# Row sums on one core: the early results leave by fifteen stores of 9, 15, 14, ... 2 partitions instead of one store of 128

## The chip, the core and the metric

The kernel runs on one core of a Trainium2 chip. Its time is the device time of one execution in microseconds (us). The kernel before takes 160.73 us, the median of three runs that lie between 160.67 and 160.77. Four engines appear below: VectorE (DVE), ScalarE (ACT), GpSimd (POOL, which does nothing here but set constants) and SyncE (SP), which issues every transfer of this kernel. The transfers themselves are carried by the core's 16 DMA engines.

## The reference

The input is 32 x 512 rows of 1024 float32 numbers, 67.1 MB. Each row is summed and the sum multiplied by 0.5, so the output has 16,384 numbers, 65.5 KB.

```python
def reference(x, multiplier):            # x: (32, 512, 1024) float32, multiplier 0.5
    return (np.sum(x, axis=-1) * multiplier).astype(np.float32)
```

## The kernel before, in words

The 16,384 rows are cut into eight blocks of 16 rows for each of the 128 partitions. In the first seven blocks a partition owns 112 rows that follow one another in memory (`own = rows - B`, lines 42 to 45), so in the output a partition's 112 results are 448 contiguous bytes. The eighth block is another part of the input, 16 rows for each partition, and its results are 64 contiguous bytes for each partition. The results of both parts lie in one tile, `res`, columns 0 to 111 and 112 to 127.

Three buffers `xb` of 8.4 MB each take the blocks in turn. SP issues the load of a block as one transfer of 128 x 64 KB (line 75, helper `load`); from the fourth block on the load waits until VectorE is done with the buffer's previous block (the semaphore `dve_done`). The first three loads are moved to the program's entry, ahead of the barrier there, by the function at the end (`start_loads_at_entry`).

VectorE sums blocks 0 to 5 with one reduction over 16 rows each (line 117) and scales the sums into `res` (line 123). Of block 6 it sums 8 rows, and ScalarE the other 8, one row at a time (`act_row`, line 82), straight into `res`. With that the 112 early columns are complete.

The last block is loaded in five pieces, all issued by SP as soon as the buffer is free (lines 139 to 148): rows 0 to 7, 8 to 12, 13 to 14, and row 15 in two parts of 608 and 416 numbers in a tile of its own, `end`. VectorE (`dve_sum`, line 92) and ScalarE share the rows. The two parts of row 15 are VectorE's: `first` (line 167) sums the first part when it has landed, `final` (line 170) adds the second part and writes the last column of `res`. `final` waits for the second part's landing and for `first` on one semaphore.

After the five loads SP waits for the early columns (lines 149 and 151: VectorE's through `dve_done`, ScalarE's through `act_done`) and issues the early store, `out_rows <- res[:, 0:own]`, 128 x 448 bytes, as one transfer (line 150). It then waits for ScalarE's last row (line 174) and for `final`, and issues the last store, `out_last <- res[:, own:]`, 128 x 64 bytes (line 175). At the end it waits for both stores (lines 179 and 180, one instruction in the trace, under line 180). The order on SP is the order in the source; no scheduler changes it. All loads and stores are issued on SP's one queue, and each has a semaphore of its own that counts to 16 when the transfer has landed.

Of the kernel before, what the change touches and what calls it, by code (L numbers as in the profile page):

```python
# [9 lines left out]
def kernel(  # L10
# [13 lines left out]
    nc = tc.nc  # L24
# [4 lines left out]
    P = nc.NUM_PARTITIONS  # L29
# [12 lines left out]
    own = rows - B  # L42
    x_rows = x_flat[0 : P * own, :].rearrange("(p c) d -> p c d", p=P)
    x_last = x_flat[P * own : N, :].rearrange("(p c) d -> p c d", p=P)
    out_rows = out_flat[0 : P * own].rearrange("(p c) -> p c", p=P)
    out_last = out_flat[P * own : N].rearrange("(p c) -> p c", p=P)

    def sbuf(name, *shape):
        return ctx.enter_context(nc.sbuf_tensor(name, list(shape), fp32)).ap()
# [4 lines left out]
    res = sbuf("res", P, rows)  # L54
# [4 lines left out]
    def sem(name):  # L59
        return nc.alloc_semaphore(name=name)  # L60

    dve_done = sem("dve_done")
    act_done = sem("act_done")
    counts = {"dve": 0, "act": 0}

    def marks(i, engine):

        s = dve_done if engine == "dve" else act_done
        i.then_inc(s, 1)
        counts[engine] += 1  # L70
        return counts[engine]
# [33 lines left out]
    for b in range(n_blocks - 1):  # L105
# [12 lines left out]
                out=sums[:, c0 : c0 + h], in_=t[:, 0:h, :], axis=mybir.AxisListType.X  # L118
# [5 lines left out]
            out=res[:, c0 : c0 + h],  # L124
            in_=sums[:, c0 : c0 + h],
# [5 lines left out]
        if h < B:  # L131
# [3 lines left out]
            early_act = marks(i, "act")  # L135
# [11 lines left out]
        for k, (to, lo, hi) in enumerate(((0, 0, cut), (at, cut, D)))  # L147
    ]
    nc.sync.wait_ge(dve_done, early_dve)
    early = nc.sync.dma_start(out=out_rows, in_=res[:, 0:own])  # L150
    early.wait_op(act_done, early_act, "sem-ge")
    early_stored = sem("early_stored")
    early.then_inc(early_stored, 16)

    on_act = {4, 5, 6, 7, 11, 12, 14}
    for k, (lo, hi) in enumerate(pieces):
# [19 lines left out]
    store.wait_op(dve_done, done, "sem-ge")  # L176
    stored = sem("stored")
    store.then_inc(stored, 16)
    nc.sync.wait_ge(early_stored, 16)
    nc.sync.wait_ge(stored, 16)  # L180

    def start_loads_at_entry(nc_):
# [61 lines left out]
```

## Time and profile before

| What | Value |
|---|---|
| Time, median of three runs | 160.73 us (160.67 to 160.77) |
| Span of the profiled execution | 159.4 us; the profile gives it no other time of its own, so what lies around the span is read as the difference to the median, 1.3 us |
| DVE busy | 119.3 us, 75% of the span |
| ACT busy | 17.3 us, 11% |
| DMA packets | 2016, 67.18 MB, mean 421 GB/s; 98.0% of 16 engines' span |
| of these under 512 B | 480 |
| Early store, SP's issue | starts at 146.96 us, 0.35 us long, landed 10.8 us after its start |
| Last store, SP's issue | starts at 157.97 us, 0.34 us long, landed 1.4 us after its start |

The span runs from the first to the last instruction that the profile shows. A transfer has two entries: the instruction on SP's queue (SPq) that issues it, some 0.35 us, and the time from there to its landing, when its semaphore is full. A transfer is carried as packets: here one packet for each partition's contiguous run and one 4-byte packet for each increment of the semaphore. Fourteen transfers of 128 packets and 16 increments make the 2016.

### The profile page before, as it was taken

To read this page: it belongs to the slowest core of one execution; us is meant where nothing else is said; L and a number is where in the kernel's file an instruction comes from. 1 tells how busy PE (TensorE), PEld (TensorE's weight loads), DVE (VectorE), ACT (ScalarE), POOL (GpSimd) and SP (SyncE) were. 2 spreads that over 40 slices of the span, in tenths; PEclk is the share of its full clock that TensorE was granted. 3 is DMA by queue.
4 is the path that set the end of the run, shared out by engine and by line. 5 is a ranking of instruction groups with operands and counts; after the bars stand their busy time and mean duration, and the time that the engine had idled before them with its cause. 6 is when DMAs were issued, how large, how long until landed. Compare 5 with 4: busy or idle time off the path is not lost.

```text
span 159.4 us, 122 instructions
## 1 busy us (share of the span) xinstructions
DVE 119.3 (75%) x35; ACT 17.3 (11%) x31; POOL 0.2 (0%) x4
## 2 busy tenths in 40 slices
DVE  0000059998699978999599995999959999598644
ACT  3000000000000000000000000000000000397954
POOL 0000000000000000000000000000000000000000
DMA  7996996996999979969969969969979799698994
GB/s 263 526 526 263 526 510 280 526 510 280 526 395 395 526 312 477 526 296 493 526 263 526 526 263 526 510 280 526 477 312 526 345 444 526 280 501 364 421 410 145
DMA packets 2016, 67.18 MB, mean 421 GB/s; under 512 B 480, under 2 KB 608, under 8 KB 736
## 3 DMA queue, kind: packets, MB, share of 16 engines
q1 hardware_dynamic: 2016, 67.18, 98.0%
HBM read 67.11 MB, written 0.07 MB: 421 GB/s over the span
## 4 chain that ended last, share of the span: by engine, by line
DMA 76%; DVE 22%; SPq 1%; issue 0%
DMA xb<-in_x_dram 51%; DMA end<-in_x_dram 25%; DVE sums L117 22%; SPq L75 1%; DVE end L92 1%; DVE res L123 0%; DVE res L92 0%
## 5 line engine op out<-in xcount | busy, mean ns | idle before, releaser
L117 DVE TENSOR_REDUCE sums<-xb 128x16 f32<-128x16384 f32 (+1 forms) x7 | 112.0, 16001 | 30.9 <-DMA xb<-in_x_dram 30.9
L82 ACT ACTIVATE xb<-xb 128x1024 f32<-128x1024 f32 x15 | 15.7, 1044 | 137.7 <-DMA xb<-in_x_dram 137.7
L92 DVE CUSTOM_DVE_ANT_0 xb<-xb 128x512 f32<-128x512 f32 x8 | 5.1, 688 | 4.9 <-DMA xb<-in_x_dram 4.9
L82 ACT ACTIVATION_READ_ACCUMULATOR xb<-xb 128x1 f32 x15 | 2.8, 186 | 0.0
L103 DVE MEMSET end<- 128x2 f32 x1 | 0.1, 60 | 2.5 <-PEq L26 2.5
L82 ACT ACT_TABLE_LOAD x1 | 1.3, 1283 | 2.4 <-PEq L26 2.4
L123 DVE TENSOR_SCALAR res<-sums 128x16 f32<-128x16 f32 (+1 forms) x7 | 1.2, 174 | 0.2
L92 DVE CUSTOM_DVE_ANT_0 end<-end 128x304 f32<-128x304 f32 (+1 forms) x2 | 0.9, 426 | 0.1
L92 DVE DVE_READ_ACCUMULATOR2_ANT res<- 128x1 f32 x9 | 0.7, 82 | 0.0
L225 POOL MEMSET const-bfloat16-1.0<- 128x1 bf16 x1 | 0.1, 102 | 0.0
L225 POOL MEMSET const-uint8-127<- 128x1 uint8 x1 | 0.1, 102 | 0.0
L225 POOL MEMSET const-float32-1.0<- 128x1 f32 x1 | 0.1, 99 | 0.0
L225 POOL MEMSET const-float32-0.0<- 128x1 f32 x1 | 0.1, 98 | 0.2 <-issue 0.2
L92 DVE DVE_READ_ACCUMULATOR2_ANT end<- 128x1 f32 x1 | 0.1, 81 | 0.0
## 6 DMA issues: line engine op xcount, KB each, us to landing
xb<-in_x_dram SPq DMA_DIRECT2D x1, 4096.0 KB, 31.2
xb<-in_x_dram SPq DMA_DIRECT2D x1, 2560.0 KB, 36.9
xb<-in_x_dram SPq DMA_DIRECT2D x1, 1024.0 KB, 38.9
end<-in_x_dram SPq DMA_DIRECT2D x1, 304.0 KB, 39.1
end<-in_x_dram SPq DMA_DIRECT2D x1, 208.0 KB, 39.2
xb<-in_x_dram SPq DMA_DIRECT2D x7, 40.8
out_dram<-res SPq DMA_DIRECT2D x1, 56.0 KB, 10.8
out_dram<-res SPq DMA_DIRECT2D x1, 8.0 KB, 1.4
```

The source lines that it names most:

```text
L75: i = nc.sync.dma_start(out=dst, in_=src)
L82: return nc.scalar.activation(out=t[:, r, :], in_=t[:, r, :], func=mybir.ActivationFunctionType.Copy, scale=mul, accum_out=res[:, col : co ...
L92: return nc.vector.tensor_tensor_reduce(out=row[:, 0:mid], in0=row[:, 0:mid], in1=row[:, mid:], scale=scale, scalar=0.0, op0=ADD, op1=ADD, ...
L103: marks(nc.vector.memset(end[:, at - 2 : at], 0.0), "dve")
L117: nc.vector.reduce_sum(out=sums[:, c0 : c0 + h], in_=t[:, 0:h, :], axis=mybir.AxisListType.X),
L123: scaled = nc.vector.tensor_single_scalar(out=res[:, c0 : c0 + h], in_=sums[:, c0 : c0 + h], scalar=mul, op=mybir.AluOpType.mult,)
L225: nc = _bacc.Bacc("TRN2", target_bir_lowering=False, num_devices=1)
```

## The change

The one early store becomes a loop of fifteen stores. Each takes the next n partitions of the same columns, with n = 9, 15, 14, 13, ... 3, 2, which adds up to 128. The first keeps the wait for ScalarE; the wait for VectorE stands ahead of the loop as before. All count up the same semaphore, and the wait at the end asks for 16 x 15 = 240. The bytes written and their addresses are the same, and nothing else in the kernel changes; VectorE, ScalarE and GpSimd have the same instructions in the same order, and SP has fourteen transfers more between the last load and the last store.

```diff
     nc.sync.wait_ge(dve_done, early_dve)
-    early = nc.sync.dma_start(out=out_rows, in_=res[:, 0:own])
-    early.wait_op(act_done, early_act, "sem-ge")
     early_stored = sem("early_stored")
-    early.then_inc(early_stored, 16)
+    early_parts = [9] + list(range(15, 1, -1))
+    assert sum(early_parts) == P
+    p0 = 0
+    for n in early_parts:
+        early = nc.sync.dma_start(
+            out=out_rows[p0 : p0 + n, :], in_=res[p0 : p0 + n, 0:own]
+        )
+        if p0 == 0:
+            early.wait_op(act_done, early_act, "sem-ge")
+        early.then_inc(early_stored, 16)
+        p0 += n
...
-    nc.sync.wait_ge(early_stored, 16)
+    nc.sync.wait_ge(early_stored, 16 * len(early_parts))
     nc.sync.wait_ge(stored, 16)
```

## The prediction

> **What bounds the kernel now.** I read the page's head and its DMA queue first, then the chain of work that ended last, in order of time, for the end of the kernel.
>
> ```profile
> span 159.4 us, 122 instructions
> ...
> q1 hardware_dynamic: 2016, 67.18, 98.0%
> ```
>
> The queue is full for 98% of the span, so the input's 67.1 MB set the time, and only what happens after the last load can be added or taken away by a store.
>
> ```profile
> 117.88 39.13 DMA end<-in_x_dram
> 157.01 0.02 issue
> 157.03 0.50 DVE end L92 x2
> 157.54 0.02 issue
> 157.56 0.38 DVE end L92
> 157.94 0.01 DVE res L92
> ```
>
> The first part of row 15 lands at 157.01 and releases `first`. `final` starts at 157.56, 0.04 us after `first` is done (157.03 + 0.50 = 157.53) and as close behind the landing of the second part (issued 0.48 us after the first part, 39.2 us to landing, so 157.5 to 157.6): the two are a tie. The last store is issued at 157.97 and lands 1.4 us later, at 159.4. The early store isn't on this chain. The next two views, the queue of SP and the issues with their landings, say how far off it is.
>
> ```profile
> SPq L149 <- DVE res L123: 28.1, 1, 28.1
> ...
> SPq L174 <- ACT xb L82: 10.1, 1, 10.1
> SPq L180 <- DMA out_dram<-res: 1.1, 1, 1.1
> SPq L175 <- DVE res L92: 0.5, 1, 0.5
> ```
>
> ```profile
> end<-in_x_dram SPq DMA_DIRECT2D x1, 304.0 KB, 39.1
> end<-in_x_dram SPq DMA_DIRECT2D x1, 208.0 KB, 39.2
> ...
> out_dram<-res SPq DMA_DIRECT2D x1, 56.0 KB, 10.8
> out_dram<-res SPq DMA_DIRECT2D x1, 8.0 KB, 1.4
> ```
>
> After issuing the early store SP is idle for 10.1 us and then 0.5 us. The store, issued at 146.96, lands 10.8 us later, at about 157.8, though the last store needs 1.4: its packets stand behind the loads on every DMA engine. Stretches of the end show the room behind them (columns: stretch and length, busy time of DVE, ACT and POOL, clock, DMA share of 16 engines, GB/s).
>
> ```profile
> 154.00:157.00 3.00, 2.40 (x8) 2.70 (x5) 0.00 (x0) 1.00 0.96 379
> 157.00:157.30 0.30, 0.27 (x1) 0.30 (x2) 0.00 (x0) 1.00 0.15 39
> 157.30:158.80 1.50, 0.60 (x4) 0.12 (x2) 0.00 (x0) 1.00 0.00 0
> 158.80:159.10 0.30, 0.00 (x0) 0.00 (x0) 0.00 (x0) 1.00 0.31 28
> ```
>
> The queue is empty from 157.3, when the early store's packets end, to 158.8, when those of the last store begin: 1.5 us in which all 16 engines do nothing.
>
> **The change, part by part.** Issuing. SP gets fourteen transfers more. The timeline has the prices:
>
> ```profile
> 116.51 1.32 SPq L75 DMA_DIRECT2D xb<-in_x_dram  x3
> 117.88 0.94 SPq L75 DMA_DIRECT2D end<-in_x_dram  x2
> 146.96 0.35 SPq L150 DMA_DIRECT2D out_dram<-res  x1
> 157.97 0.34 SPq L175 DMA_DIRECT2D out_dram<-res  x1
> ```
>
> An issue that stands alone takes 0.35 us, one in a row 0.44 to 0.47 (0.94 / 2). Fifteen take between 15 x 0.35 = 5.3 and 15 x 0.47 = 7.1 us; I take the latter, since they stand in a row, and SP is through at 146.96 + 7.1 = 154.0. Queued behind them on SP is only the wait of line 174, which ends with ScalarE's last row at 157.4, and the last store, due at 157.97. The cover is 3.4 us to the first; it would be gone at (157.97 - 146.96) / 15 = 0.73 us for one issue. Cost 0.
>
> Room for what is issued. By the trace's packets, when the fifth piece had been issued at 118.82, 848 packets were queued and not started, 53 on each engine, in six transfers. With the change the load of rows 13 and 14 and the two parts of row 15 are still queued at 154.0, at most 27 packets on each engine, and on top come 128 stores' packets and at most 240 increments, 23 for each engine if evenly spread: 50. So the packets fit in what was held before; the number of transfers, 18 against six or seven, was never tried here. Cost 0, and a rival.
>
> Packets. On the engine that ends last, the trace has the early store's packets of 448 bytes 21 ns apart and an increment 6 ns ahead of what follows. Eight and one increment took 8 x 21 + 6 = 174 ns. How a store of 9 or 15 partitions is laid on the engines no row shows. Evenly, nothing but the increments grows. If every store takes one packet on each engine from the same first one, the fullest engine has fifteen of each: 15 x 27 = 405 ns, 0.23 more. If all went to one engine, 128 x 21 + 15 x 6 = 2.8 us, from 157.1 to 159.9, 1.1 us past the start of the last store's packets. I take 0.23, because all fourteen transfers of the trace are spread over the engines (224 increments, 16 for each); it lies in the 1.5 us of empty queue. Less than before isn't to be had, since those packets aren't on the chain. Cost 0, at worst 1.1.
>
> The Trainium skill, DMA: Bandwidth & Descriptors, section "Why a DMA increments its semaphore by 16 and not by 1", says that a transfer uses the largest number of engines up to 16 that divides its outer dimension, the lowest-numbered ones. By that rule the fullest engine has fifteen stores' packets and engines post 128 increments; the sum is the same. No run here shows it yet.
>
> Landing of the loads. The last increments of row 15's second part hold up `final`, and the fifteen stores put up to 128 increments, if one per packet, beside them instead of 16. The landings in the trace bound the price. The last store's sixteen increments land exactly 10 ns apart, though several were issued within 3 ns; around the early store no two, of store or load, land less than 11 ns apart; but those of earlier loads come as little as 3 ns apart. If all pass through one line at 12 ns in the order of issue, replaying the packets with fifteen to none on the engines puts the last load's increment 0.1 to 0.53 us later, by which engine ends last. If the engines take turns, 15 x 12 = 0.18 us is the most. If the counter takes one in 3 ns, nothing. The straggler's load increment landed 0.43 us after its packet in the midst of store increments that took 0.52, so it did not stand behind them all: I take 0.05 us, near the lower end, and keep 0 and 0.53.
>
> The end. The last wait now asks for 240. Issued packets end by about 157.5 and increments land by 158.8 even at 12 ns each, before the last store's at 159.4. Cost 0; the 1.3 us around the span are unchanged.
>
> Sum, against the profiled execution's 159.43 us of span and 1.30 us to the median of the runs: 159.43 + 1.30 + 0 + 0 + 0 + 0.05 + 0 = 160.78 us. No difference under 0.2%, 0.32 us, can be told from no change here.
>
> **The rivals.** (1) The crowd of increments, the other side: with one line at 10 to 12 ns in order of issue, `final` and the last store start 0.32 to 0.53 us late, 161.05 to 161.26. It decides from about 27 increments (0.32 / 0.012) ahead of the straggler's. For it: the spacing above; against it: the straggler's 0.43 us. (2) Stores that go one at a time on an engine, each waiting for its increment to land. The trace has 0.50 us from the straggler's increment packet of the early store to its landing. Fifteen take 7.5 us from 157.0, so the last store's packets start at 164.5 instead of 158.8: 166.4. It decides from (158.8 - 157.0) / 15 = 0.12 us for one. Against it: after a load's increment the next packet starts 6 ns later, and an early store's increment was issued 175 ns after a load's on the same engine while that was in flight. The Trainium skill, Perfetto Trace Analysis, section "DMA Instruction — HWDGE (DVE, Sync)", says that the increment waits for the write and that this can be surprisingly long towards HBM; the trace agrees only in part, 0.50 for the store against 0.43 for the load. (3) A limit on transfers in flight. With four loads still out at 147.7 and each landing setting one free, a limit of 15 or more costs nothing; at eight, seven stores are issued only after 157.9, 7 x 0.35 to 0.44, so 2.5 to 3.1 us: 163.2 to 163.8. (4) A short store's issue costs more than 0.73 us; at 1.0 SP is through at 162.0, 4 us late: 164.8. (5) Faster: the straggler carries less behind its loads. But its loads stand ahead of the stores, and if its two last landings came with the other engines', about 0.15 us sooner, `first` would still wait for VectorE's row before, which ends at 156.97, and gain 0.06, `final` 0.04 more: 160.63, within the 0.2%. More than that needs a shorter landing of the last store, which no row suggests.
>
> **How the numbers follow.** The forecast and the small gain of (5) together 0.63, own range 160.6 to 161.0; (1) 0.17; (2) 0.05; (3) 0.07; (4) 0.02; a gain over 0.32 us by something unseen 0.06. Same 0.63, slower 0.31, faster 0.06. The range 160.5 to 161.4 holds the forecast's cases and (1) with its upper bound, 0.80.
>
> **What the profile after would show.** Fifteen issues on SP from 146.96, 0.35 to 0.47 each, through by 154; SP's wait for ScalarE's last row still there, some 3 us; the last store's issue within 0.1 us of 157.97 and 1.4 us to landing; more packets under 512 B. Against me: an issue of the last store after 158.3 with `final` late (1) or SP busy until then (3, 4), or a landing of the last store over 1.7 us after its issue (2).

## The result, and the profile after

The kernel with fifteen stores takes 161.75 us, the median of four runs (161.63 to 162.0), against 160.74 us for the kernel before: a ratio of 1.0065, 95% interval 1.005 to 1.0079. It is 1.0 us slower. The profiled execution took 161.79 us; its span is 160.5 us, 1.05 longer than before.

The page of the changed kernel: the queue carries 112 packets more, which are increments (128 for the fifteen stores, where the one had 16).

```profile
span 160.5 us, 136 instructions
...
DMA packets 2128, 67.18 MB, mean 419 GB/s; under 512 B 592, under 2 KB 720, under 8 KB 848
...
q1 hardware_dynamic: 2128, 67.18, 97.4%
```

The end of its chain of work, in order of time (start, length, what):

```profile
117.80 39.10 DMA end<-in_x_dram
156.89 0.02 issue
156.91 0.51 DVE end L92 x2
157.42 0.02 issue
157.45 0.38 DVE end L92
157.82 0.01 DVE res L92
```

Nothing is late up to here. The two parts of row 15 land as before, and `final` is done 0.12 us earlier than before, which is the spread of two executions. Its timeline and the issues with their landings (last column) show SP's side:

```profile
146.84 5.43 SPq L155 DMA_DIRECT2D out_dram<-res  x15
...
157.86 0.36 SPq L183 DMA_DIRECT2D out_dram<-res  x1
```

```profile
out_dram<-res SPq DMA_DIRECT2D x1, 8.0 KB, 2.6
```

SP is through with the fifteen stores at 152.3 and issues the last store at 157.86. But this store, with the same 8 KB, lands 2.6 us after its issue instead of 1.4. That is the whole loss: -0.11 for the earlier issue, +1.16 for the later landing, 1.05 together. The queue of SP says the same as a wait:

```profile
SPq L182 <- ACT xb L82: 5.1, 1, 5.1
SPq L188 <- DMA out_dram<-res: 2.2, 1, 2.2
SPq L183 <- DVE res L92: 0.5, 1, 0.5
```

The wait at the end was 1.1 us and is 2.2. The last view is the one that decides. In stretches of the end (DVE, ACT, POOL busy, clock, DMA share, GB/s) the DMA engines are hardly busier than before (a share of 0.23 against 0.15 in the first stretch, then none as before):

```profile
157.00:157.30 0.30, 0.30 (x1) 0.30 (x2) 0.00 (x0) 1.00 0.23 48
157.30:158.70 1.40, 0.48 (x4) 0.01 (x1) 0.00 (x0) 1.00 0.00 0
158.70:159.00 0.30, 0.00 (x0) 0.00 (x0) 0.00 (x0) 1.00 0.31 28
159.00:160.50 1.50, 0.00 (x0) 0.00 (x0) 0.00 (x0) 1.00 0.00 0
```

The packets of the early stores end at 157.30, and those of the last store start at 158.71 and end at 158.92. Then no packet moves for 1.5 us, and the kernel waits. What is late isn't data but the increments of the semaphores. The trace records when each one lands. The last packet of an early store's increment started at 157.30, but the last of these increments landed at 160.25; the last increment of the last store landed at 160.43. From 159.3 on the landings come in groups of six, six, five, three, one and one, 0.18 to 0.21 us from the start of one group to the next. That fits engines that each land one increment, then the next, and drop out as their number is used up.

### The profile page after: what moved, and what is told of

Same layout as the page of the kernel before. It is cut to its first block, busy times and chain, and to the rows that moved or that the text cites. A ratio compares the mean times of both kernels' runs of the same rounds, so it can differ in the third digit from the quotient of the medians.

```text
span 160.5 us, 136 instructions
## 1 busy us (share of the span) xinstructions
DVE 119.3 (74%) x35; ACT 17.3 (11%) x31; POOL 0.2 (0%) x4
## 2 busy tenths in 40 slices
DMA packets 2128, 67.18 MB, mean 419 GB/s; under 512 B 592, under 2 KB 720, under 8 KB 848
## 3 DMA queue, kind: packets, MB, share of 16 engines
q1 hardware_dynamic: 2128, 67.18, 97.4%
## 4 chain that ended last, share of the span: by engine, by line
DMA 75%; DVE 22%; SPq 1%; issue 0%
DMA xb<-in_x_dram 51%; DMA end<-in_x_dram 24%; DVE sums L117 21%; SPq L75 1%; DVE end L92 1%; DVE res L123 0%; DVE res L92 0%
## 6 DMA issues: line engine op xcount, KB each, us to landing
end<-in_x_dram SPq DMA_DIRECT2D x1, 304.0 KB, 39.1
end<-in_x_dram SPq DMA_DIRECT2D x1, 208.0 KB, 39.1
xb<-in_x_dram SPq DMA_DIRECT2D x7, 40.8
```

## The experiments

The theory after the result, called the chain: a DMA engine lands its increments one after another, some 0.19 us each, so the engine with most of them sets when the last store has landed. The rivals are a crowd (all increments in one line), a counter (increments of one semaphore in line) and a wait that only writes to HBM have.

All runs at a glance. In the run with fifteen semaphores each store of n partitions, from 2 to 15, has n landings beside one that comes within 0.2 us of the end of SP's issue, so it runs on n engines. "Fullest" is the number of early increments on the fullest engine, if all stores start from the same first engine; the trace doesn't name the engines. The times are medians, the ratios are to the kernel before on the same chip; the landings are from the profiled execution.

| Run | Fullest | Last early increment landed | Last store landed | Time, us | Ratio, 95% interval |
|---|---|---|---|---|---|
| before | 1 | 157.78 | 159.39 | 160.74 | |
| eight of 16 | 8 | 159.32 | 159.53 | 160.83 | 1.0002, 0.9993 to 1.0012 |
| eleven | 11 | 159.60 | 159.78 | 161.08 | 1.0012, 1.0003 to 1.002 |
| the change | 15 | 160.25 | 160.43 | 161.75 | 1.0065, 1.005 to 1.0079 |
| fifteen, own semaphores | 15 | 159.96 | 160.14 | 161.52 | 1.0048, 1.0033 to 1.0063 |
| fifteen loads | 16 | 160.23 | 160.41 | 161.83 | 1.0062, 1.0046 to 1.0079 |
| sixteen of 8 | 16 | 160.66 | 160.86 | 162.31 | 1.0097, 1.008 to 1.0114 |
| sixteen halves | 16 | 160.92 | 161.12 | 162.45 | 1.0102, 1.0087 to 1.0117 |
| halves, own semaphores | 16 | 160.60 | 160.81 | 162.29 | 1.0087, 1.0073 to 1.0101 |
| thirty-two of 4 | 32 | 163.29 | 163.47 | 164.79 | 1.0251, 1.0235 to 1.0266 |

The row of fifteen loads counts the loads and the one store.

**Other numbers of stores.** Three runs change one line of the change, a fourth was made later:

```diff
-    early_parts = [9] + list(range(15, 1, -1))
+    early_parts = [16] * 8                 # eight of 16
+    early_parts = [8] * 16                 # sixteen of 8
+    early_parts = [4] * 32                 # thirty-two of 4
+    early_parts = [16] * 7 + [4] * 4       # eleven
```

> Eight stores of 16 partitions instead of fifteen of 9, 15, ... 2. Both have 128 increments posted by engines, but the fullest engine has 8 of them here and 15 in the change. Chain (my theory now: an engine lands the increments of its stores one after another, about 0.19 us each, so the fullest engine's number sets when the last store lands): the last early increment at 157.2 + 8 x 0.19 = 158.7 us, before the last store's own at 159.2, so no cost: 160.75, 160.65 to 160.95. Crowd (all increments of stores pass through one line, 128 of them in the 2.98 us seen after, 23.5 ns each): as the change, 161.7.

> Sixteen stores of 8 partitions: 128 increments again, if a store of n partitions runs on n engines then 16 on each of eight engines and none on the others. Chain: the last early increment at 157.2 + 16 x 0.19 = 160.25 us, the last store's on the same engines 0.19 later: 161.75, 161.6 to 162.1. Crowd: 161.7 as the change. This run separates the two little and gives the chain its second point.

> Thirty-two stores of 4 partitions: 128 increments, 32 on each of four engines if n partitions use n engines. SP issues them in 32 x 0.30 to 0.35 us, through by 156.4 to 158.0, so the last store's issue is late by 0.1 at most. Chain: 157.2 + 32 x 0.19 = 163.3 us, the last store's increments 0.19 later, 163.5 against 159.4 before: 164.8 us, 164.2 to 165.6. Crowd: the number of increments is that of the change, 161.7.

All three have the change's 128 increments, and the times go with the fullest engine: 160.83, 162.31 and 164.79 us. The issues of eight of 16 and then of thirty-two of 4 show it in the landing of the same last store:

```profile
out_dram<-res SPq DMA_DIRECT2D x1, 8.0 KB, 1.5
```

```profile
out_dram<-res SPq DMA_DIRECT2D x1, 8.0 KB, 5.4
```

The crowd, which gave 161.7 for all three, is out. The chain met the times of the eight and the thirty-two and missed the sixteen by 0.56 us. There the steps were longer: eight engines at work together to the end took 0.21 us for a step, and I had taken 0.19 from a kernel in which the engines drop out one by one. The landings of the eight were late by as much, 159.32 us instead of 158.7, but still ahead of the last store's, so that its time hid it.

In thirty-two of 4 more than increments wait. Two stretches of its end, after SP's last early issue (157.83):

```profile
157.90:158.90 1.00, 0.12 (x2) 0.00 (x0) 0.00 (x0) 1.00 0.54 10
160.30:163.50 3.20, 0.00 (x0) 0.00 (x0) 0.00 (x0) 1.00 0.00 0
```

Where the change has an empty queue, packets of the early stores are still under way here, at 10 GB/s. By the packet records they start in steps of 0.185 us on four engines, until 159.7, and the last store's last data packet starts only at 160.24. From 157.5 to 160.1 some 72 increments are posted and not landed, 18 for each of the four engines. So with about 18 increments in flight an engine starts the next store's packets only as one of them lands; in the change, with at most fifteen, no packet waited.

> Eleven stores, seven of 16 partitions and four of 4: the fullest four engines have 11 increments, all engines together 128. Chain at 0.18 to 0.22 us for each (0.18 was the step of the fifteen stores with semaphores of their own, 0.22 that of the sixteen of 8): the last early increment lands at 157.2 + 11 x 0.18 to 0.22 = 159.2 to 159.6 us, the last store's on those engines one step later, 159.4 to 159.8, against 159.4 before: the point from which it begins to cost, 160.75 to 161.15, most likely 160.9. Crowd by the total of 128 alone, which eight of 16 and thirty-two of 4 have spoken against: 161.7.

Eleven takes 161.08 us against 160.86 beside it, a loss of 0.2 us (ratio 1.0012, 1.0003 to 1.002). So the loss begins between eight and eleven. From eleven to thirty-two, both with four engines to the end, the last early increment moves by 163.29 - 159.60 = 3.69 us for 21 increments: 0.176 us each.

**One semaphore or fifteen.**

```diff
-        early.then_inc(early_stored, 16)
+        early_sems.append(sem(f"early_stored{p0}"))
+        early.then_inc(early_sems[-1], 16)
...
-    nc.sync.wait_ge(early_stored, 16 * len(early_parts))
+    for s in early_sems:
+        nc.sync.wait_ge(s, 16)
```

> The change with a semaphore of its own for each of the fifteen stores, and fifteen waits at the end. Counter (a rival: increments of one semaphore are what stands in line): no line any more, 160.75. Chain: the line is in the engine, not in the semaphore, so 161.7 as the change, 161.5 to 162.0.

161.52 us: the counter, which gave 160.75, is out as the cause. This run also shows the chain most clearly, because each store's landing can be told from the next one's. The last increments of the first eight stores landed at 157.68, 157.86, 158.05, 158.23, 158.41, 158.59, 158.77 and 158.95 us, and of the last two at 159.78 and 159.96, though SP had issued the fifteen up to 5.2 us apart and their packets had all ended by 157.42. That is 0.18 us for a step. A part of 0.3 us may belong to the counter: with one semaphore the last early increment lands at 160.25 instead of 159.96. The early increments of the change land no closer than 11 ns, while here some come 3 ns apart, even two of the same store (159.955 and 159.958). What sets that distance stays open.

**More increments on all engines.** The stores are cut to 16 partitions x 56 columns, two for each 16 partitions, 256 increments with 16 on every engine; then the same with sixteen semaphores.

```diff
-    early_parts = [9] + list(range(15, 1, -1))
+    early_parts = [(16, h) for _ in range(8) for h in (0, 1)]
...
-    for n in early_parts:
+    for n, h in early_parts:
+        cols = slice(h * half, (h + 1) * half)
         early = nc.sync.dma_start(
-            out=out_rows[p0 : p0 + n, :], in_=res[p0 : p0 + n, 0:own]
+            out=out_rows[p0 : p0 + n, cols], in_=res[p0 : p0 + n, cols]
         )
```

> Sixteen stores of 16 partitions x 56 columns: 256 increments posted by engines instead of 128, 16 on every engine. Chain, with a fixed wait per increment: 16 on the fullest engine as with sixteen of 8: 161.75, 161.6 to 162.1. Crowd, one line for all: 256 x 23.5 ns = 6.0 us from 157.3, 164.7; at the 12 ns that is the least distance of two landings, 256 x 12 = 3.1 us from 157.3, 160.4, so at least 161.7.

> The sixteen stores of 16 partitions x 56 columns with a semaphore of its own for each: 256 increments, 16 on every engine. One counter takes increments 12 ns apart, several take them 3 to 6 ns apart (after, and fifteen with semaphores of their own). If that distance is what made sixteen of 16 x 56 cost 0.7 us more than a step of 0.19 says: the last early increment at 157.2 + 16 x 0.18 = 160.1, the last store's at 160.3: 161.6, 161.4 to 161.9. If the step grows with the number of engines at work, whichever counter: 162.45, as with one semaphore.

162.45 and 162.29 us. Twice the increments of sixteen of 8 cost 0.14 us more, with ratios whose intervals overlap, so it is the fullest engine that counts and not the sum; the 164.7 of the crowd is out again. My explanation of what the time had over the forecast failed too: semaphores of their own took only 0.16 us of it away. In the run with sixteen semaphores the last landings of one store and the next are 0.17 to 0.22 us apart, and the engine whose loads end last now has a chain as long as the others'. It lands its last load's increment at 157.57, and 157.57 + 16 x 0.19 = 160.6 is what was measured there (0.19 is the mean step of this same run, so this is a reading and not a test). I had started every chain at 157.2. With one semaphore the landing is 0.3 us later, 160.92; that rest isn't explained.

**Loads instead of stores.** The one early store stays, and fifteen loads of the same sizes stand behind it, into a tile that nothing reads.

```diff
+    for n in extra_parts:
+        more = nc.sync.dma_start(
+            out=extra[p0 : p0 + n, :], in_=x_rows[p0 : p0 + n, 0, 0:own]
+        )
+        more.then_inc(extra_landed, 16)
+        p0 += n
```

> The early store is one of 128 again, and behind it stand fifteen loads of 9, 15, ... 2 partitions x 448 bytes from the input into a tile that nothing reads: as many short transfers and increments as in the change, but written to SBUF. Chain of stores (each increment waits for a write to HBM to be confirmed): loads don't form the chain, 160.75, 160.65 to 161.0. Chain of any increments: 161.7. The 57 KB of extra reads cost 16 packets of 21 ns for each engine behind the last load, nothing on the chain.

161.83 us, as much as the stores. The wait at SP's end and the last store's landing in this kernel:

```profile
SPq L190 <- DMA extra<-in_x_dram: 1.6, 1, 1.6
```

```profile
out_dram<-res SPq DMA_DIRECT2D x1, 8.0 KB, 2.2
```

So the time isn't a matter of writes to HBM alone. Transfers into SBUF form the same chain.

**The last store on another queue.**

```diff
-    nc.sync.wait_ge(act_done, late_act)
-    store = nc.sync.dma_start(out=out_last, in_=res[:, own:])
+    nc.scalar.wait_ge(act_done, late_act)
+    store = nc.scalar.dma_start(out=out_last, in_=res[:, own:])
```

> The change with the last store issued by ScalarE, on its own queue, after its last row. Chain within one queue only: the last store's increments land 1.4 us after the issue, about 159.3, and SP then waits for the early stores' last increment at 160.25: span 160.3. Chain of the DMA engine whatever the queue: the last store lands behind the early stores' increments as in the change, 160.4.

One execution: 161.71 us, span 160.4, and the issue on ScalarE's queue:

```profile
out_dram<-res ACTq DMA_DIRECT2D x1, 8.0 KB, 2.4
```

Issued at 157.92, it landed at 160.34, 0.18 us after the early stores' last increment at 160.16. So the line stands in the DMA engine, and another engine's queue doesn't pass it. The Trainium skill, DMA: Bandwidth & Descriptors, section "Queues, rings and completion order", has the rule: a semaphore's increment is a strongly ordered write and lands only after every earlier write from that DMA engine, on whichever queue. This run and the loads agree; the 0.18 us that each takes is the runs' number.

**The same stores 20 us earlier.** Columns 0 to 63 are complete at 97.4 us. Here the fifteen stores take those columns, 256 bytes for each partition, and are issued then, between the load of block 6 and the pieces of the last block; their packets run at 137.0 to 137.5 us, behind block 6. Columns 64 to 111 leave in one store where the early store was.

```diff
+    nc.sync.wait_ge(dve_done, freed[3] + 1)
+    p0 = 0
+    for n in early_parts:
+        part = nc.sync.dma_start(
+            out=out_rows[p0 : p0 + n, 0:64], in_=res[p0 : p0 + n, 0:64]
+        )
+        part.then_inc(early_stored, 16)
+        p0 += n
...
-    early = nc.sync.dma_start(out=out_rows, in_=res[:, 0:own])
+    early = nc.sync.dma_start(out=out_rows[:, 64:], in_=res[:, 64:own])
```

> The fifteen stores take columns 0 to 63, which are ready at 97.4 us, and are issued then, ahead of the five pieces of the last block; columns 64 to 111 leave in one store where the early store was. The same fifteen increments on the fullest engine, but with 20 us of loads behind them. Chain: the 3 us of it pass while the last block is loaded, the last store lands 1.4 us after its issue: 160.75, up to 161.1 if the fullest engine's fifteen packets and increments, 0.4 us, delay its loads. If fifteen stores cost 1 us wherever they stand: 161.7.

162.32 us, ratio 1.0091 (1.0076 to 1.0106): more than the change itself, where I had expected next to nothing. The issues of this kernel, the last two pieces of row 15 and the last store:

```profile
end<-in_x_dram SPq DMA_DIRECT2D x1, 304.0 KB, 40.8
end<-in_x_dram SPq DMA_DIRECT2D x1, 208.0 KB, 40.8
...
out_dram<-res SPq DMA_DIRECT2D x1, 8.0 KB, 1.4
```

The last store is back at 1.4 us, so the chain is over by then; but the loads land 1.6 to 1.7 us later than before (40.8 against 39.1 and 39.2). Where they lose it shows in one stretch, first of this kernel, then of the kernel before:

```profile
137.50:138.50 1.00, 0.61 (x1) 0.62 (x1) 0.00 (x0) 1.00 0.65 165
```

```profile
137.50:138.50 1.00, 0.53 (x1) 0.53 (x1) 0.00 (x0) 1.00 0.68 295
```

The view counts a packet's bytes where the packet starts, so 165 against 295 GB/s means that five packets of 32 KB start in this microsecond instead of nine. By the packet records the first packets of the last block's first load took 1.7 to 2.4 us on eight engines, and 1.21 to 1.25 on the others. Its sixteen increments in order of landing, each against the one of the same place before, come 0.2 to 0.3 us later for the first seven, then 0.6 for one, 1.0 for two, 1.4 to 1.5 for four and 1.6 to 1.7 for two. If all stores start from the same first engine, seven engines have 6 stores or fewer, one has 8, two have 9 and 10, four have 11 to 14 and two have 15: the same numbers of engines, in the same order. My reading is that an engine whose increments have piled up is held from further data. To see whether that or the number of transfers is at work, two runs put eight and four stores there:

```diff
-    early_parts = [9] + list(range(15, 1, -1))
+    early_parts = [16] * 8                 # eight before the last block
+    early_parts = [32] * 4                 # four before the last block
```

> As the fifteen stores ahead of the last block, but eight of 16 partitions, so eight increments on every engine. Held engine (a DMA engine whose increments have piled up starts no further load): with fifteen the load of the first piece landed late by 1.65 us on two engines, which by the layout have 15 stores, by 0.4 us on one, which would have 8, and by nothing on seven, which would have 6 or fewer. Here all engines have 8, so the loads end 0.4 us late: 161.15, 160.95 to 161.5, although the same eight stores cost nothing at the end. If only the fifteen transfers in SP's way cost there (SP stood 16.3 us in one issue): SP has seven fewer to issue, is not held, and 160.75.

161.5 us against 160.86, ratio 1.0037 (1.0024 to 1.005). The same number of stores that cost nothing at the end costs 0.6 us ahead of the loads, and the landings of row 15's pieces are late again:

```profile
end<-in_x_dram SPq DMA_DIRECT2D x1, 304.0 KB, 39.9
end<-in_x_dram SPq DMA_DIRECT2D x1, 208.0 KB, 39.9
```

The 0.4 us was too little, but SP's way isn't the cause: SP stood in none of its issues in this run. On every engine the second packet of the last block's first load is slow, 1.52 to 1.84 us, and on most the first is too, up to 1.52.

> Four stores of 32 partitions x 64 columns ahead of the last block, four increments on every engine where the run before had eight and lost 0.6 us. Held engine with room for some six increments (the engines that by the layout had six stores or fewer lost nothing with the fifteen): four fit, the loads aren't held, 160.85, 160.75 to 161.0. If every transfer ahead of the loads costs its share, 0.6 / 8 = 0.08 us for one: 4 x 0.08 = 0.3, 161.15.

160.94 us against 160.82, ratio 1.0006 (0.9997 to 1.0015). Four increments per engine can't be told from none, and the same load packets take 1.21 to 1.25 us. A share of 0.08 us for each transfer would have been 0.3 us, a ratio of 1.002, which the interval leaves out. So four increments on an engine do the loads behind them no measurable harm, and eight do. That held data are the mechanism is argued from these packets and not shown; why eight are enough ahead of large loads, where thirty-two of 4 reached 18 before a small store's packets waited, stays open.

**Not tried.** In every run each transfer posts increments; none has a long row of transfers without them. The step may belong to the increment or to the end of a transfer; the runs don't separate the two.

## Why the prediction was wrong

- **Issuing: right in its cost of 0.** Fifteen issues took 5.43 us in all, near the lower of the two bounds and not the 7.1 of the sum; single ones took 0.25 to 0.38 us. SP was through at 152.3 with 5.1 us to spare.
- **Room for what is issued: right here.** SP stood in none of the fifteen issues, nor in thirty-two; rival 3 and rival 4 cost nothing in this place.
- **Packets: right.** They ended at 157.30, inside the empty queue. The Trainium skill, DMA: Bandwidth & Descriptors, section "Why a DMA increments its semaphore by 16 and not by 1", has the rule by which the engines post 128 increments; the trace agrees: 2016 - 16 + 128 = 2128 packets.
- **Landing of the loads: right within 0.05.** `final` started 0.03 us behind `first`, as before; the crowd of rival 1 didn't reach it. One row was misread on the way: the last store's increments of before land 10 ns apart but for the last, which is 26 ns behind.
- **The end: the step that failed.** It said that the increments land by 158.8 us, "even at 12 ns each", before the last store's. I took 12 ns, about the least distance of two landings around the early store, as the price of an increment. At most that is the distance between increments of different engines. On one engine the price is 0.18 to 0.2 us, and the fullest engine has fifteen: the last landed at 160.25, not by 158.8, and the last store's stood behind it and landed 2.6 us after its issue instead of 1.4. The term of the end, put at a cost of 0, was 1.16 us.
- **Rival 2 was the mechanism, mis-sized and on the wrong object.** It said that stores wait for one another on an engine at 0.50 us each, gave 166.4 us and had a chance of 0.05. The runs show 0.18 for a step, not 0.50, since a step isn't the whole way from a packet to its landing; and with the change's fifteen stores the increments wait, not the stores' packets. The prediction had it decide from 0.12 us for one, which is below the 0.18 measured, and the sign named for it, a last landing more than 1.7 us after the issue, is what came. The evidence that I set against it, the next packet 6 ns behind an increment, is true and says nothing on this: packets do run past increments in flight, until some 18 have piled up in thirty-two of 4, where the stores' packets wait as well.
- **A number that I had read otherwise.** In the trace of before, the straggler's load increment and early-store increment were posted 175 ns apart and landed 245 ns apart. I put the extra 0.07 us down to the write to HBM. A step of the chain, 0.18 to 0.21, may be in it as well, and the run with loads speaks for that reading; it isn't shown. With 0.2 us for a step rival 2 would have given 157.4 + 15 x 0.2 = 160.4 for the early stores and 160.6 for the last one, a time of 161.9.
- **Rival 5, a gain: none seen.** No run was faster than the kernel before.

## What to carry to other kernels

Count how many transfers end on one DMA engine at about the same time, not only their bytes and packets: here each cost 0.18 to 0.21 us in landing order on that engine, and the last transfer of the kernel stood behind all of them, even from another queue (one execution). Eight were hidden by the 1.5 us that the last results needed anyway, eleven were not. Moving such a row of small transfers ahead of large loads didn't hide it: the loads behind eight of them landed some 0.7 us later and those behind fifteen up to 1.7 us, while four cost nothing that could be measured.

## What the runs showed that I had not expected

- Loads into SBUF pay the same step as stores to HBM (161.83 against 161.75 us).
- An idle DMA queue isn't a finished one: the windows show a share of 0.00 for 1.5 us while increments land.
- With fifteen stores ahead of the last block, SP stood 16.3 us in one issue, that of the last piece:

```profile
117.86 16.80 SPq L75 DMA_DIRECT2D end<-in_x_dram  x2
```

Some limit on what may be queued was met there. It isn't a number of transfers alone, since with thirty-two of 4 some thirty were queued at once and no issue took longer than 0.36 us. It cost nothing that shows: the last piece's landing is late by no more than that of the pieces issued without a wait. What the limit counts stays open.
